# Another order for the first stage of a two-layer diffusion transformer: modulation, norm and first products ahead of the filters' taps and spectra, sums of squares in PSUM

## The chip, the core and the metric

The kernel runs on one core of a Trainium2 chip, in one launch. The metric is device time in microseconds (us), the median of 3 runs. Besides TensorE (PE; its weight loads are listed as PEld), the core has VectorE (DVE), ScalarE (ACT), GpSimd (POOL) and SyncE (SP), which here only issues DMAs. Each engine works through its own instructions in order and waits on semaphores. TensorE reads operands from SBUF and writes to eight banks of PSUM.

## The reference, cut to what matters

Two layers work on 256 latent tokens and 256 context tokens of 1024 features. What the first stage of the kernel computes is the beginning of layer 0 and the filters of both layers' long convolutions:

```python
cond_lat = jax.nn.silu(c)
cond_ctx = jax.nn.silu(c_ctx)[None]
m = adaln(cond_lat, ada_w[l], ada_b[l])        # 9 vectors of 1024: shift, scale, gate, ...
h = h + 0.5 * m[2] * swiglu(modulate(rms_norm(h), m[0], m[1]), ffn1_up[l], ffn1_down[l])
# rms_norm: x * rsqrt(mean(x * x) + eps); modulate: x * (1 + scale) + shift

# hyena_filter: a sine network of three layers, then taps, a window and a norm
hdn = jnp.sin(f_freq[0] * (z @ f_w1 + f_b[0]))
hdn = jnp.sin(f_freq[1] * (hdn @ f_w_mid[0] + f_b[1]))
hdn = jnp.sin(f_freq[2] * (hdn @ f_w_mid[1] + f_b[2]))
filt = (hdn @ f_w_out).reshape(length, 2, HY_W) * jnp.exp(-t * deltas)[:, None, :]
k_full = ...                                   # both directions
return k_full / jnp.sum(jnp.abs(k_full), axis=0, keepdims=True)
# fft_conv multiplies by rfft(k_full), the filter's spectrum
```

After that come the feed-forward block, four token mixers, a gated merge and a second feed-forward block, and all of it again for layer 1.

## The kernel before

Features lie on the partitions (8 tiles of 128), the 512 tokens of both streams along the free axis. A matrix product in full precision is made of three products (`mm3`, lines 250 to 252): weights and activations are split into a high part of reduced mantissa (`whi`, `nh`) and the remainder (`wlo`, `nl`). ScalarE casts the high part and VectorE subtracts for the low one (lines 224 and 225). Filters, sums and modulation use plain fp32 operands instead; every such product is recorded as two matmul records, two passes.

The first stage is the method `start`. It has five strands:
- **The filters' network** (`filter_layer`, lines 527 to 543): three small layers for both depths at once. Each is one product on TensorE, six operations on VectorE, and a sine on ScalarE.
- **Taps and spectra** (`filter_list`): per depth four taps (line 551; VectorE multiplies by the window, line 553), their sums and differences (`e`, line 562), five spectra of two products each (line 583; ScalarE copies them to `K`, line 585, and stores them to DRAM from its own queue, line 588), and the norm of the taps: absolute values on ScalarE (line 569), sums on GpSimd (line 571), four products with ones (line 574). `K` has two buffers.
- **Sums of squares**: ScalarE squares the eight feature tiles (line 1219), GpSimd adds them into `acc` (line 1221), and TensorE sums over partitions with four products by a column of ones (line 352). VectorE scales (line 344), GpSimd raises to the power -1/2 (line 345), and four products with the identity spread the factor over the partitions (line 357).
- **Modulation units** (`ada_unit`): 256 modulation columns each, from 1 MB of weights (`araw`, line 281). Eight narrow products (line 285), a copy (line 288), two products that add up the four partial sums (line 291), then the bias on VectorE (line 322). Units 4 to 7 make scales, units 0 to 3 shifts. The units 4+p and p belong to pair p of feature tiles.
- **Normalisation and first products**: `norm_pair` for pair p multiplies by the factor (`nt`, line 369), applies scale and shift on ScalarE (`nh`, line 374) and GpSimd (`nv`, line 375), and takes the difference on VectorE (`nl`, line 376). `mm3` then adds pair p's share to the two accumulators of the first feed-forward tile (`lead`): 24 products after p = 1 (pairs 0 and 1), 12 after p = 2 and 12 after p = 3.

In the code, the taps of both depths come first, and the spectra are written last. A scheduler places each engine's instructions by its own estimate of when their operands are ready, so the engine's sequence is not the code's; the sequences shown below are what it put out. PSUM's eight banks are shared out by kind: three for matmul (`mmb`), two for scores and spectra (`sb`), two for small results (`ptb`), one for unit sums (`ob`). SyncE issues the loads in the order of its own sequence, and a load waits for the buffer that it fills and for an earlier load's semaphore.

## Time and profile before

| | |
|---|---|
| median of 3 runs | 2556.85 us (2555.41 to 2559.32) |
| span of the profiled execution | 2554.3 us |
| TensorE busy | 2483.0 us, 97% of the span |
| VectorE, ScalarE, GpSimd busy | 59%, 39%, 13% |
| chain that ended last | PE 9%, issue 8%, DVE 2%, the rest 1% each or less |

The page has no time of the profiled execution other than its span; the span runs from the first to the last instruction. A busy share is an average: of the page's 40 slices (64 us each), all but the first show TensorE busy at 8 tenths or more, and the first shows 6. For that slice one looks at the engines' timelines. The page's clock digits are tenths of the full clock as far as the profiler has records of it.

### The profile page before, as it was taken

How to read it: one execution, taken by the hardware profiler on the slowest of the kernel's cores; microseconds unless marked ns; L12 is line 12 of the kernel's file. 1: busy time of each engine (PE TensorE's matmuls, PEld its weight loads, DVE VectorE, ACT ScalarE, POOL GpSimd, SP SyncE). 2: the span in 40 equal slices, each digit the busy share in tenths (PEclk: the TensorE clock that was granted, in tenths of full speed). 3: DMA queues.
4: the chain of work that ended last, by engine and by line, in shares of the span. 5: the costliest groups of instructions: out<-in, count | busy, mean ns of one | idle time of the engine just before them, and what ended most of it. 6: DMA issues, size and time to landing. Idle time of an engine off the chain costs nothing. (4 is left out here: it accounts for less than half of the span.)

```text
span 2554.3 us, 35123 instructions
## 1 busy us (share of the span) xinstructions
PE 2483.0 (97%) x13980; PEld 2092.7 (82%) x13980; DVE 1501.3 (59%) x2404; ACT 1004.1 (39%) x1767; POOL 320.7 (13%) x378
## 2 busy tenths in 40 slices
PE   6999999999999999999999999999999999899998
PEld 3788888876887777688888888888898898789998
DVE  5779865465465345557785355553356765556555
ACT  3422224455235434434222233222236545445443
POOL 3100001111113122212000010000021122221000
PEclk9999999999999999999999999999999999999999
DMA  7556544132212243333564234452243433545453
GB/s 268 207 182 229 190 167 147 57 92 81 97 38 87 64 108 91 102 123 139 187 219 168 73 133 182 163 199 92 81 141 108 160 124 91 124 130 189 148 202 113
DMA packets 82907, 350.99 MB, mean 137 GB/s; under 512 B 25206, under 2 KB 31032, under 8 KB 56632
## 3 DMA queue, kind: packets, MB, share of 16 engines
q1 hardware_dynamic: 81016, 345.61, 40.9%
q10 hardware_dynamic: 1728, 3.15, 0.3%
q8 instruction: 110, 1.80, 0.3%
q14 instruction: 53, 0.43, 0.1%
HBM read 333.52 MB, written 6.82 MB: 133 GB/s over the span
## 5 line engine op out<-in xcount | busy, mean ns | idle before, releaser
L250 PE MATMUL mmb<-nh,whi 128*128 128x512 f32 (+1 forms) x2224 | 788.5, 355 | 2.8 <-ACT nh L374 1.4
L251 PE MATMUL mmb<-nl,whi 128*128 128x512 f32 (+1 forms) x2224 | 786.0, 353 | 2.8 <-DVE nl L376 2.8
L252 PE MATMUL mmb<-nh,wlo 128*128 128x512 f32 (+1 forms) x2224 | 787.0, 354 | 1.1 <-DVE wlo L225 0.9
L224 ACT CAST whi<-raw 128x1024 fp32r<-128x1024 f32 (+4 forms) x532 | 474.3, 925 | 728.4 <-PE mmb L251 632.0
L225 DVE TENSOR_TENSOR wlo<-raw,whi 128x1024 fp32r<-128x1024 f32 (+4 forms) x532 | 582.3, 1117 | 151.7 <-ACT whi L224 134.5
L250 PEld LDWEIGHTS mmb<-nh,whi 128*128 128x128 f32 x2224 | 422.1, 190 | 65.6 <-issue 6.8
L251 PEld LDWEIGHTS mmb<-nl,whi 128*128 128x128 f32 x2224 | 421.9, 190 | 63.0 <-DVE nl L376 5.4
L252 PEld LDWEIGHTS mmb<-nh,wlo 128*128 128x128 f32 x2224 | 421.7, 190 | 63.0 <-issue 4.9
L251 PE MATMUL mmb<-pl,whi 128*128 128x512 f32 (+1 forms) x770 | 267.1, 347 | 0.0
L252 PE MATMUL mmb<-ph,wlo 128*128 128x512 f32 (+1 forms) x770 | 267.1, 347 | 0.0
L250 PE MATMUL mmb<-ph,whi 128*128 128x512 f32 (+1 forms) x770 | 266.8, 347 | 0.0
L430 DVE TENSOR_TENSOR s<-s,mmb 128x512 f32<-128x512 f32 (+1 forms) x85 | 52.7, 620 | 239.8 <-PE mmb L252 232.0
L314 DVE SCALAR_TENSOR_TENSOR vraw<-vraw,cb 128x1024 f32<-128x1024 f32 x128 | 155.6, 1224 | 36.2 <-DMA vraw<-in_adat 29.2
L345 POOL TENSOR_TENSOR rstd<-msq,nhalf 128x2 f32<-128x2 f32 (+1 forms) x11 | 8.4, 764 | 1308.5 <-DVE msq L344 1308.5
L251 PEld LDWEIGHTS mmb<-pl,whi 128*128 128x128 f32 x770 | 145.8, 189 | 18.2
L250 PEld LDWEIGHTS mmb<-ph,whi 128*128 128x128 f32 x770 | 145.8, 189 | 18.1
L252 PEld LDWEIGHTS mmb<-ph,wlo 128*128 128x128 f32 x770 | 145.8, 189 | 17.9
L314 DVE SCALAR_TENSOR_TENSOR scr<-vraw,cb 128x1024 f32<-128x1024 f32 x96 | 117.2, 1221 | 42.5 <-DMA vraw<-in_adat 36.9
L386 DVE SCALAR_TENSOR_TENSOR h<-mmb,mods,h 128x256 f32<-128x256 f32 x136 | 61.3, 480 | 129.9 <-PE mmb L252 129.8
L741 POOL TENSOR_SCALAR P<-P,rs 128x512 f32<-128x512 f32 (+1 forms) x144 | 92.2, 657 | 319.2 <-DVE rs L738 286.4
L429 ACT ACTIVATE s<-mmb 128x512 f32<-128x512 f32 (+1 forms) x85 | 46.3, 545 | 212.1 <-PE mmb L252 212.1
L252 PE MATMUL mmb<-whi,nl 128*128 128x256 f32 (+1 forms) x400 | 113.6, 284 | 0.9 <-DVE nl L376 0.7
(269 smaller groups left out, 3461.0 us busy)
## 6 DMA issues: line engine op xcount, KB each, us to landing
raw<-in_up SPq DMA_DIRECT2D x88, 1024.0 KB, 4.9
vraw<-in_adat SPq DMA_DIRECT2D x64, 1024.0 KB, 4.9
raw<-in_wmg SPq DMA_DIRECT2D x64, 768.0 KB, 4.5
raw<-in_dn SPq DMA_DIRECT2D x64, 704.0 KB, 4.1
raw<-in_wh SPq DMA_DIRECT2D x12, 1024.0 KB, 4.9
araw<-in_adaw SPq DMA_DIRECT2D x8, 1024.0 KB, 9.1
K<-K SPq DMA_DIRECT2D x64, 128.0 KB, 2.7
raw<-in_wnqk SPq DMA_DIRECT2D x8, 1024.0 KB, 4.9
```

The lines of the kernel that those rows point to most:

```text
L224: nc.scalar.copy(hi, src)
L225: nc.vector.tensor_tensor(lo, src, hi.bitcast(F32), ALU.subtract)
L250: nc.tensor.matmul(out, wh, xh, start=start and i == 0, stop=False)
L251: nc.tensor.matmul(out, wh, xl, start=False, stop=False)
L252: nc.tensor.matmul(out, wl, xh, start=False, stop=stop and i == n - 1)
L314: nc.vector.scalar_tensor_tensor(out, raw[:, j], 1.0, self.cb[:, s], ALU.mult, ALU.mult, accum_out=mc[:, j, s:s + 1])
L345: nc.gpsimd.tensor_tensor(out, ms[:, :n], self.nhalf[:, :n], ALU.pow)
L386: self.nc.vector.scalar_tensor_tensor(h[:, j, a:b], ps[:, a:b], self.mods[l][:, 8 * chunk + j, g:g + 1], h[:, j, a:b], ALU.mult, ALU.add)
L429: nc.scalar.activation(s[:, :n], pa[:, :n], AF.Silu)
L430: nc.vector.tensor_tensor(s[:, :n], s[:, :n], pg[:, :n], ALU.mult)
L741: nc.gpsimd.tensor_scalar(sl, sl, rs[:, qt:qt + 1], 0.0, ALU.mult, ALU.add)
```

## The change

The method `start` is written in another order, and three helpers are cut to fit it.
- The sums of squares no longer pass through GpSimd: each squared tile is multiplied by the column of ones at once, and the eight tiles add up in one bank of PSUM (32 products where there were 4). `rstd_bcast` is split, so that `start` can call its second half, `rstd_spread`, on that bank.
- The factor is spread before any taps. The modulation units of pair 0 follow, its normalisation, then the taps of depth 0, then pair 1 with the first products, and so on; taps and spectra of depth 1 come last. The two depths now share the taps' buffers (`f`, `e` without the depth in their name).
- Loads: the units' weights have four buffers of their own. The first two stand right behind the activations, the next two behind the taps' weights, then the first up weights and the table for the spectra. The constants of layer 1 are loaded last.

```diff
-    def ada_unit(self, i, u, pool, bufs):
+    def ada_load(self, i, pool, bufs):
         raw = pool.tile([128, 2048], F32, tag="raw", name="araw", bufs=bufs)
         r = raw.rearrange("p (k c) -> p k c", k=8)
-        nc.sync.dma_start(out=r, in_=self.a["adaw"][i])
+        self.nc.sync.dma_start(out=r, in_=self.a["adaw"][i])
+        return r
+
+    def ada_unit(self, r, u, pool):
...
-        ev = self.cp.tile([128, 256], F32, tag="adaev", name="adaev", bufs=2)
+        ev = pool.tile([128, 256], F32, tag="adaev", name="adaev", bufs=2)
...
+        return self.rstd_spread(wk, st, nb)
+
+    def rstd_spread(self, wk, st, nb):
...
-            f = fp.tile([128, 512], F32, name=f"f{l}{i}{d}")
+            f = fp.tile([128, 512], F32, name=f"f{i}{d}")
...
-                    st["eo"[q], i] = t = fp.tile([128, 512], F32, name=f"e{l}{i}{q}")
+                    st["eo"[q], i] = t = fp.tile([128, 512], F32, name=f"e{i}{q}")
...
         for j in range(0, KT, 2):
-            nc.sync.dma_start(out=h[:, j:j + 2], in_=self.a["xt"][:, j:j + 2])
+            nc.sync.dma_start(out=h[:, j:j + 2], in_=a["xt"][:, j:j + 2])
+        nc.sync.dma_start(out=self.small[0], in_=a["small"][0])
+        units = _ada_units()[0]
+        raws = [self.ada_load(i, sp, 4) for i in (4, 0)]
         self.filter_load_taps(fp, c)
-        for l in range(L):
-            nc.sync.dma_start(out=self.small[l], in_=self.a["small"][l])
+        raws += [self.ada_load(i, sp, 4) for i in (5, 1)]
         for i in range(3):
             self.filter_layer(fp, c, i)
+        st = self.tbank()
         for j in range(KT):
-            sq = sp.tile([128, T], F32, tag="sq", name="sq", bufs=2) if j else acc
+            sq = sp.tile([128, T], F32, tag="sq", name="sq", bufs=2)
             nc.scalar.activation(sq, h[:, j], AF.Square)
-            if j:
-                nc.gpsimd.tensor_tensor(acc, acc, sq, ALU.add)
-        fl = [f for pair in zip(*(self.filter_list(fp, l, c) for l in range(L))) for f in pair]
-        self.do(fl[:8])
-        units = _ada_units()[0]
+            for b in range(T // 128):
+                nc.tensor.matmul(st[:, b:b + 1], sq[:, 128 * b:128 * b + 128], self.ones[:, 0:1],
+                                 start=j == 0 and b == 0, stop=j == KT - 1 and b == T // 128 - 1)
+        bc = self.rstd_spread(wk, st, T // 128)
+        fl = [f for l in range(L) for f in self.filter_list(fp, l, c)]
         for p in range(4):
-            self.ada_unit(4 + p, units[4 + p][1], sp, 2)
-            self.ada_unit(p, units[p][1], *((self.wp, 3) if p % 2 else (sp, 2)))
-            if p == 0:
-                self.filter_load_dft(fp, c)
-                bc = self.rstd_bcast(wk, acc, 0, T)
             if p == 1:
-                wh, wl = self.load(self.a["up1"][0, 0], [2, 8, 128])
+                wh, wl = self.load(a["up1"][0, 0], [2, 8, 128])
                 lead = [self.bank(), self.bank()]
+                self.filter_load_dft(fp, c)
+            for i in (4 + p, p):
+                raw = raws.pop(0)
+                if p < 2:
+                    raws.append(None)
+                self.ada_unit(raw if raw is not None else self.ada_load(i, sp, 4), units[i][1], sp)
             for g, x, y in self.groups(T):
                 self.norm_pair(wk, bc[:, x:y], h, 0, 0, g, x, y, 2 * p)
+            self.do(fl[:4] if p == 0 else ())
             if p == 0:
-                self.do(fl[8:10])
                 continue
...
-        self.do(fl[10:])
+            self.do(fl[4 * p:4 * p + 4])
+        nc.sync.dma_start(out=self.small[1], in_=a["small"][1])
+        self.do(fl[16:])
         return [lead]
```

How this moves instructions on the engines shows in their sequences. The lines of the changed kernel are a few higher for the same operation. TensorE, from the last tap on, before: units are `ob`, spectra `sb<-e`, sums `ptb<-ones,acc`, the spread `ptb<-ident,rstd`.

```order
L551 MATMUL mmb<-fwo,hdn_171 128x512
L285 MATMUL ob<-araw,cond 32x256 x8
L583 MATMUL sb<-e_301,fdft 128x512
L291 MATMUL ptb<-ident,adaev 128x2 x2
L285 MATMUL ob<-araw,cond 32x256 x8
L583 MATMUL sb<-e_305,fdft 128x512
L291 MATMUL ptb<-ident,adaev 128x2 x2
L352 MATMUL ptb<-ones,acc 128x1 x4
L583 MATMUL sb<-e_309,fdft 128x512
L357 MATMUL ptb<-ident,rstd 128x128 x4
L583 MATMUL sb<-e_313,fdft 128x512
```

Seven more taps stand ahead of these rows. TensorE from its first product on, after (`ptb<-ones,sq` are the sums, `sb<-hdn` the filter layers, `mmb<-fwo` the taps):

```order
L535 MATMUL sb<-fzt,fw_118 128x256
L1233 MATMUL ptb<-ones,sq 128x1 x8
L535 MATMUL sb<-hdn,fwm 128x256
L1233 MATMUL ptb<-ones,sq 128x1 x16
L535 MATMUL sb<-hdn,fwm 128x256
L1233 MATMUL ptb<-ones,sq 128x1 x8
L365 MATMUL ptb<-ident,rstd 128x128 x4
L288 MATMUL ob<-araw,cond 32x256 x8
L294 MATMUL ptb<-ident,adaev 128x2 x2
L288 MATMUL ob<-araw,cond 32x256 x8
L294 MATMUL ptb<-ident,adaev 128x2 x2
L559 MATMUL mmb<-fwo,hdn_175 128x512 x4
```

The sums, now eight times as many, stand between the filter layers; the spread and two units come ahead of the first tap, and four of the eight taps are left for later.

TensorE around the first products (`mmb<-nh,whi`), before:

```order
L285 MATMUL ob<-araw,cond 32x256 x8
L583 MATMUL sb<-e_313,fdft 128x512
L291 MATMUL ptb<-ident,adaev 128x2 x2
L583 MATMUL sb<-e_303,fdft 128x512
L250 MATMUL mmb<-nh,whi 128x512
L251 MATMUL mmb<-nl,whi 128x512
L583 MATMUL sb<-e_307,fdft 128x512
L252 MATMUL mmb<-nh,wlo 128x512
L250 MATMUL mmb<-nh,whi 128x512
L251 MATMUL mmb<-nl,whi 128x512
```

The same place after:

```order
L288 MATMUL ob<-araw,cond 32x256 x8
L294 MATMUL ptb<-ident,adaev 128x2 x2
L288 MATMUL ob<-araw,cond 32x256 x8
L294 MATMUL ptb<-ident,adaev 128x2 x2
L591 MATMUL sb<-e_390,fdft 128x512
L250 MATMUL mmb<-nh,whi 128x512
L251 MATMUL mmb<-nl,whi 128x512
L252 MATMUL mmb<-nh,wlo 128x512
L250 MATMUL mmb<-nh,whi 128x512
L251 MATMUL mmb<-nl,whi 128x512
```

Before, ten products for spectra (`sb<-e`) stand ahead of or among the first 24 products; after, one. The first products now follow the second pair of units directly.

ScalarE ahead of the casts of the first weights (`whi`), before:

```order
L585 ACTIVATE K<-sb,kw 128x512 x2
L288 COPY adaev<-ob 128x256
L588 DMA kd_101<-K 128x512
L588 DMA kd_100<-K 128x512
L288 COPY adaev<-ob 128x256
L224 CAST whi<-raw 128x1024 x2
L374 ACTIVATE nh<-nt,mods_95 128x256 x4
```

The same after (`as` and `ab` are the absolute values of the taps):

```order
L291 COPY adaev<-ob 128x256
L577 ACTIVATE ab<-f_301 128x512
L291 COPY adaev<-ob 128x256
L382 ACTIVATE nh<-nt,mods_95 128x256 x3
L224 CAST whi<-raw 128x1024 x2
L382 ACTIVATE nh<-nt,mods_95 128x256
L593 ACTIVATE K<-sb,kw 128x512
```

Before, the casts stand ahead of the pair's four activations; after, behind three of them.

## Rows read from the trace of the kernel before

**Rows 1.** Windows: stretch, length, TensorE busy (records), clock, DMA share, GB/s.

```profile
0.00:21.94 21.94, 3.64 (x7) 1.00 0.87 316
21.94:40.15 18.21, 17.06 (x78) 0.96 0.49 171
```

**Rows 2.** Timeline of TensorE: start, duration, line, operation, shapes, records, idle before.

```profile
9.20 1.22 PE L527 MATMUL sb<-hdn,fwm 128*128 128x256 f32 x2 [4.16 <-ACT hdn L538]
21.94 8.67 PE L551 MATMUL mmb<-fwo,hdn 128*128 128x512 f32 x16 [3.93 <-ACT hdn L543]
30.54 1.07 PE L285 MATMUL ob<-araw,cond 128*32 128x256 f32 x16
35.71 1.03 PE L352 MATMUL ptb<-ones,acc 128*128 128x1 f32 x8
36.60 1.10 PE L583 MATMUL sb<-e,fdft 128*128 128x512 f32 x2
38.48 1.88 PE L357 MATMUL ptb<-ident,rstd 128*128 128x128 f32 x8 [0.77 <-POOL rstd L345]
49.07 0.80 PE L250 MATMUL mmb<-nh,whi 128*128 128x512 f32 x1
56.62 0.40 PE L252 MATMUL mmb<-nh,wlo 128*128 128x512 f32 x1
```

**Rows 3.** Timeline of TensorE's weight loads during the taps.

```profile
22.95 0.34 PEld L551 LDWEIGHTS mmb<-fwo,hdn 128*128 128x128 f32 x1 [0.52 <-issue]
25.29 0.19 PEld L551 LDWEIGHTS mmb<-fwo,hdn 128*128 128x128 f32 x1 [0.30 <-issue]
25.72 0.19 PEld L551 LDWEIGHTS mmb<-fwo,hdn 128*128 128x128 f32 x1 [0.24 <-issue]
```

**Rows 4.** Windows of TensorE around two falls of the clock.

```profile
36.00:38.70 2.70, 1.93 (x11) 1.00 1.01 413
38.70:42.10 3.40, 3.40 (x11) 0.50 0.99 373
2346.10:2350.00 3.90, 2.21 (x8) 0.50 0.40 90
```

**Rows 5.** Timeline of TensorE, a late sum at the lower clock.

```profile
2346.54 0.99 PE L352 MATMUL ptb<-ones,acc 128*128 128x1 f32 x4 [2.71 <-DVE acc L339]
```

**Rows 6.** Timeline of ScalarE, VectorE and GpSimd in the first stage.

```profile
7.70 0.63 ACT L1219 ACTIVATE acc<-h 128x512 f32<-128x512 f32 x1 [3.09 <-DMA h<-in_xt]
16.32 0.42 ACT L538 ACTIVATE hdn<-sx 128x256 f32<-128x256 f32 x1 [2.78 <-DVE sx L535]
41.12 2.08 ACT L374 ACTIVATE nh<-nt,mods 128x256 fp32r<-128x256 f32 x4 [4.88 <-DVE nt L369]
...
5.08 0.54 DVE L530 TENSOR_SCALAR sx<-sb,fbf 128x256 f32<-128x256 f32 x1 [3.26 <-PE sb L527]
7.24 0.29 DVE L535 TENSOR_SCALAR sx<-sx 128x256 f32<-128x256 f32 x1
10.46 0.54 DVE L530 TENSOR_SCALAR sx<-sb,fbf 128x256 f32<-128x256 f32 x1 [2.94 <-PE sb L527]
...
37.02 1.40 POOL L345 TENSOR_TENSOR rstd<-msq,nhalf 128x4 f32<-128x4 f32 x1 [3.97 <-DVE msq L344]
41.19 2.70 POOL L375 TENSOR_SCALAR nv<-nt,mods 128x256 f32<-128x256 f32 x4 [2.77 <-DVE nt L369]
```

**Rows 7.** Timeline of SyncE's queue, and the modulation loads' time to landing.

```profile
7.69 1.59 SPq L281 DMA_DIRECT2D araw<-in_adaw  x2
...
DMA to landing us min/median/max: 5.3/9.1/11.1
```

**Rows 8.** Timeline: casts and low halves of the first weights.

```profile
47.61 2.00 ACT L224 CAST whi<-raw 128x1024 fp32r<-128x1024 f32 x2
...
48.79 2.36 DVE L225 TENSOR_TENSOR wlo<-raw,whi 128x1024 fp32r<-128x1024 f32 x2
```

**Rows 9.** Waits of the first 110 us: us, times, longest.

```profile
ACT K L585 <- DMA kd<-K: 4.6, 3, 2.0
```

More of the change, by code (lines that the diff above doesn't have):

```diff
@@ L273, in tbank @@
         return self.pt.tile([128, 512], F32, tag="pt", name="ptb")
-    def ada_unit(self, i, u, pool, bufs):
-        nc = self.nc
+    def ada_load(self, i, pool, bufs):
         raw = pool.tile([128, 2048], F32, tag="raw", name="araw", bufs=bufs)
         r = raw.rearrange("p (k c) -> p k c", k=8)
-        nc.sync.dma_start(out=r, in_=self.a["adaw"][i])
+        self.nc.sync.dma_start(out=r, in_=self.a["adaw"][i])
+        return r
+    def ada_unit(self, r, u, pool):
+        nc = self.nc
         ps = self.obank()
@@ L352, in rstd_bcast @@
             nc.tensor.matmul(st[:, j:j + 1], acc[:, a + 128 * j:a + 128 * j + 128], self.ones[:, 0:1], start=True, stop=True)
+        return self.rstd_spread(wk, st, nb)
+    def rstd_spread(self, wk, st, nb):
+        nc = self.nc
         rs = wk.tile([128, 16], F32, tag="rstd", name="rstd", bufs=2)
@@ L358, in rstd_bcast @@
                              start=True, stop=True)
-        return tb[:, :b - a]
+        return tb[:, :128 * nb]
     def groups(self, n):
@@ L1223, in start @@
-        self.do(fl[:8])
-        units = _ada_units()[0]
+            for b in range(T // 128):
[3 more added lines that the diff above has]
+        fl = [f for l in range(L) for f in self.filter_list(fp, l, c)]
         for p in range(4):
-            self.ada_unit(4 + p, units[4 + p][1], sp, 2)
-            self.ada_unit(p, units[p][1], *((self.wp, 3) if p % 2 else (sp, 2)))
-            if p == 0:
+            if p == 1:
+                wh, wl = self.load(a["up1"][0, 0], [2, 8, 128])
+                lead = [self.bank(), self.bank()]
```

4 lines of the change are left out of this document (1 added, 3 removed).

## The prediction, made before the changed kernel had run

> **What bounds the kernel now.** First the page's shares: TensorE is busy for 97% of the span, so a change of the first stage can only win what TensorE idles there, and must not give it work. The windows of the first stage [rows 1] show the idle time: of the first 21.94 us TensorE works 3.64, of the next 18.21 it works 17.06. The timeline [rows 2] shows what it does: three layers of the filter network with long gaps, eight taps at 21.94, the modulation units from 30.54, the sums of squares at 35.71, the spread of the norm's factor at 38.48 to 40.36, the first products of the first feed-forward tile from 49.07. The last of the first 24 of these starts at 56.62 and the next row at about 56.9. From there nearly every slice is full, so I measure the change by that place: when do these 24 products end, and how much of the first stage's TensorE work is then still to come. TensorE's order after the first stage is the same in both kernels.
>
> **The clock comes into every price.** In the first 25 us TensorE runs at its lower level, 1.2 GHz: the same weight load takes 0.34 us at 22.95 and 0.19 at 25.29 [rows 3]. The window row of that stretch still prints a clock of 1.00 [rows 1]; the durations are to be believed. Later the granted clock reads 0.50 from 38.70 to 42.10 and again from 2346.10 [rows 4]. It rose at about 25 after 3 us of dense taps. It fell at 38.70 after a stretch in which TensorE had run mostly one-column products, one product for a spectrum and then idled.
>
> **What the sums of squares cost on TensorE.** Before, the eight squares are added on GpSimd and TensorE makes 4 products of one column (8 records). After, each of the eight squares gets its 4 products: 32, or 64 records. At the full clock a record takes 0.111 us: eight start at 35.71 and the next row at 36.60 [rows 2]. At the lower clock, four take 0.99 with their tail [rows 5]; the tail at the full clock is 1.03 - 0.89 = 0.14, so a record is (0.99 - 0.14)/4 = 0.2125; the nearest other row, the spread at 38.48 (128 columns out, nearly all at clock 0.50), takes 1.88 for eight, at most 0.235 each. The bounds for all 64 are thus 7.1 and 15.0 us. I take 13.6: they run from 8 to 24 us, where the clock is low now, and they are the very kind of product after which it fell. It is neither less than zero nor hidden: in before, these 8 records cost 0.9.
>
> The Trainium skill ("TensorE: Matmul & The Clock Gate", section "LDWEIGHTS (loading the stationary operand)") prices a weight load by its columns over 1.2, 107 ns for 128, with no second price for the lower clock. By it the 64 would cost 6.8 us and the sum below would come out near +2 us. The row at 2346.54 speaks for twice that; I keep the row, and the other outcome is the first rival.
>
> **The path after, step by step** (lower clock until the taps).
> 1. The first square is ready at 7.70 + 0.6 [rows 6]; the sums start at 8.4. TensorE takes 13.6 for them and two filter layers of 1.1 each between them: end 24.2. A square's buffer (two of them) is free as soon as its four products are done, so ScalarE keeps ahead.
> 2. The seven GpSimd additions go, and with them, as I read it, the slowdown of VectorE beside them: the second layer's chain took from 10.46 to its sine at 16.32, the first, undisturbed, 5.08 to 7.5 [rows 6]. It wins nothing: ScalarE's second sine now stands behind four squares that wait for TensorE, and comes at about 17.4 instead of 16.3.
> 3. Mean square 0.2, power on GpSimd 1.40 [rows 6], spread 1.88 [rows 2]: the factor is there at 27.9 instead of 40.4. That is the gain of the reorder, 12.5 us.
> 4. Two modulation units. A unit is 1.07 us at the full clock [rows 2], then ScalarE's copy and the way there 0.6, then 4 records, 0.45. At the lower clock I take 2.1 + 0.6 + 0.85, twice: 27.9 + 7.1 = 35.0. Their loads stand two places earlier in the queue than now; now they are issued at 7.69, and no unit's load took longer than 11.1 us to land [rows 7], so none is late.
> 5. Four taps, layer 0. A pass is 0.85 at the lower clock and 0.43 at the full one (25.29 to 25.72 [rows 3]); eight passes between 3.4 and 6.8, with the clock rising after some 3 us as at 25: 5.6. End 40.6. The first pair's normalisation (GpSimd 2.70 [rows 6]) lies beside them.
> 6. Two more units at the full clock, 2.1 each: 44.7, modulation columns ready at 45.0.
> 7. ScalarE's order puts three of the pair's four activations (2.08 for four [rows 6]) ahead of the two casts of the first weights (2.00 [rows 8]): first half cast at 47.6, second 48.6. VectorE has a difference and a product ahead of its two (2.36 for both): 49.1 and 50.3.
> 8. The products start at 47.6, where before it was 49.07; eight can run before the second low half is there, the other 16 take 16 x 0.23 = 3.7: end at 54.2. So the first products end 2.7 us **earlier** than now.
> 9. But TensorE has less behind it. Before that point it now has done all eight taps and ten products for spectra, each of two passes; after the change four taps and one product for spectra. Thirteen products of 0.86 move behind it: +11.2 us.
>
> Sum: -2.7 + 11.2 = +8.5. Bounds of this case: clock up already at the units -1 to -3; gaps where TensorE waits for the last low difference or a modulation column +0 to +1.5. So +5.5 to +10 by this walk, and I take +8.7. The same by work and idle: TensorE gets +12.7 for the sums, about +2.9 for two units at the lower clock and +0.4 for the taps; spectra that now run between 38.70 and 42.10 at the lower clock save about 1; it idles some 15.5 us up to the 24 products instead of 19.5 (18.3 and 1.15 by [rows 1]): +11. So +11 is this case's upper end.
>
> **At no cost:** the moved loads. On SyncE's queue the first up weights and the spectra's tables now stand ahead of the load that waits for the first unit's products (done at 30); with 11.1 us to land [rows 7] they are there by 41, and their first users come at 44.7 and 46.6. That cover is thin: a load later by 10 us would cost TensorE 5 at the first products. Taps of layer 1 now reuse layer 0's buffers and wait for its spectra; two further units and 12 products stand between.
>
> **Rivals.**
> - *The sums run at 0.111 a record.* Either the clock rises early in them or the weight loads don't follow the clock. The Trainium skill (same page, section "What's actually happening") says activity releases the throttle, and by that the unbroken stream of sums could release it. For it: TensorE is issuing nearly without a gap from 8.4 on. Against it: at 38.70 the clock fell right after such records. It would save 6.5 us on the sums, and, with the clock still up, up to 6 more on spread, units and taps: Δ from +2.2 down to -3.8, about 2553 to 2559. It decides from five of the eight squares on at the full clock (each saves 0.81, 4.1 in all): then the result is no longer slower beyond what can be measured.
> - *The clock falls a second time, and spectra wait for their stores.* Between 44.7 and 50.3 TensorE has one product for a spectrum and half of its first products; a like stretch ended in a fall at 38.70. Then 3.4 us run at half rate: +1.7. And layer 0's five spectra now follow one another, with two buffers whose stores ScalarE now waits for 3 times, 4.6 us in all, at most 2.0 [rows 9]; one copy of a modulation unit stands behind such a wait: 0 to +3. Together +10.5 to +13.5: 2567.3 to 2570.3.
> - *The reorder does as it looks*: first products early enough that TensorE idles much less (under 8 us up to the first products) and the time falls by over 0.2%. The gaps of steps 4 and 7 would have to vanish as well as half of the sums: the full-rate case's -3.8, less 2.4 for the copies' gaps of step 4 and 2.2 for step 7, is -8.4 or 2548.4. I see no row for it.
>
> **How the numbers follow.** The profiled span is 2554.3; the median is 2556.85, 2.55 above it (what lies around the span and run to run). 2554.3 + 8.7 + 2.55 = 2565.5. Chances: this case 0.60, second fall and stores 0.17, full-rate sums 0.19, the last 0.04. The measurement can tell about 0.2%, 5.1 us, from no change. This case lies above that except for its lower edge (0.03): slower 0.60 - 0.03 + 0.17 = 0.74; same 0.03 + 0.18 = 0.21; faster 0.05. The range reaches down to 2557, into the full-rate case (two thirds of it, 0.13, and the last case stay out), and up to 2569.5, over most of the second-fall case.
>
> **What would show it.** Right: 64 one-column records of 0.21 us between 8 and 24.5; the spread's end near 28; the first products at 47 to 48.5 and the 24th near 54; the first stage's TensorE rows then ending some 9 us later than now. Wrong at step 1 if the records are 0.11 apart; at step 4 or 5 if the weight loads read 0.19 before the taps; at step 7 if the casts come before the third activation's modulation columns; at step 9 if TensorE has gaps behind the first products. If the profile shows the sums hidden in time that TensorE idled anyway, with the factor at 20 instead of 28, the first rival holds.

## The result, and the profile after

The changed kernel takes **2570.88 us** (median of 4 runs, 2570.13 to 2572.41) against 2556.72 of the kernel before (4 runs, 2555.41 to 2559.32): ratio 1.0057, 95% interval 1.0045 to 1.0069, 14.2 us slower. Forecast was 2565.5 with a range of 2557.0 to 2569.5: the sign was right, the size was not, and the time lies above the range. The profiled spans are 2569.5 and 2554.3.

To find where the time comes in, take one product that both kernels have behind all of the filters' work: the 83rd product of the feed-forward block. It starts at 87.76 in before and at 102.22 after, 14.5 us later; from there on the difference stays between 14.0 and 16.3, and is 15.2 at the end. So the first stage has nearly all of it. I call this product **the mark**.

Windows of before, cut at its first tap, first product, end of the 24th product and the mark (length, TensorE busy with records, weight loads, VectorE, ScalarE, GpSimd, clock, DMA share, GB/s):

```profile
0.00:21.94 21.94, 3.64 (x7) 1.50 (x7) 12.06 (x23) 7.26 (x14) 9.13 (x11) 1.00 0.87 316
21.94:49.07 27.13, 25.98 (x131) 13.29 (x131) 16.83 (x32) 10.73 (x20) 8.34 (x9) 0.94 0.51 180
49.07:56.85 7.78, 7.08 (x28) 4.79 (x26) 5.15 (x7) 3.77 (x7) 4.58 (x4) 1.00 1.01 410
56.85:87.76 30.91, 30.43 (x176) 19.90 (x175) 12.89 (x23) 16.29 (x27) 9.55 (x11) 1.00 0.61 225
```

The same four of after:

```profile
0.00:34.02 34.02, 24.40 (x118) 20.34 (x119) 9.49 (x28) 8.61 (x16) 1.20 (x5) 1.00 0.83 311
34.02:49.22 15.20, 10.29 (x51) 4.36 (x51) 11.67 (x20) 7.68 (x15) 9.33 (x11) 0.82 0.68 256
49.22:57.24 8.02, 7.92 (x24) 5.90 (x25) 3.61 (x4) 1.40 (x2) 0.20 (x1) 0.71 0.17 71
57.24:102.22 44.98, 42.42 (x202) 24.71 (x200) 19.73 (x33) 20.55 (x34) 9.91 (x11) 1.00 0.49 176
```

Read the last rows first. The first products start at the same time (49.22 against 49.07) and the 24th ends 0.4 later; but behind it stand 202 records and not 176, 42.42 us of work and not 30.43. These 26 records are the thirteen products of the filters that the change moved behind. TensorE's idle time up to the mark (length less busy) falls only from 20.6 to 17.2 us, although 12.8 us of sums were put into the first window.

TensorE after, in order of time, for [rows 2, 5]:

```profile
8.48 3.58 PE L1233 MATMUL ptb<-ones,sq 128*128 128x1 f32 x16 [3.63 <-ACT sq L1231]
12.91 6.83 PE L1233 MATMUL ptb<-ones,sq 128*128 128x1 f32 x32
20.59 3.41 PE L1233 MATMUL ptb<-ones,sq 128*128 128x1 f32 x16
25.35 2.08 PE L365 MATMUL ptb<-ident,rstd 128*128 128x128 f32 x8 [1.35 <-POOL rstd L348]
27.36 1.94 PE L288 MATMUL ob<-araw,cond 128*32 128x256 f32 x16
...
34.02 5.07 PE L559 MATMUL mmb<-fwo,hdn 128*128 128x512 f32 x8
39.02 1.07 PE L288 MATMUL ob<-araw,cond 128*32 128x256 f32 x16
...
43.82 2.06 PE L591 MATMUL sb<-e,fdft 128*128 128x512 f32 x2
49.22 0.80 PE L250 MATMUL mmb<-nh,whi 128*128 128x512 f32 x1 [3.35 <-ACT whi L224]
...
57.01 0.40 PE L252 MATMUL mmb<-nh,wlo 128*128 128x512 f32 x1
...
79.21 1.13 PE L559 MATMUL mmb<-fwo,hdn 128*128 128x512 f32 x2 [0.85 <-DVE f L561]
...
84.22 0.50 PE L251 MATMUL mmb<-nl,whi 128*128 128x512 f32 x1 [1.71 <-DVE nl L384]
```

The sums take 0.21 us a record (6.83/32), the factor is spread at 27.43, the taps end at 39.09. At 43.82, behind the second pair's units, a product for a spectrum takes 2.06 us where it took 1.10 in [rows 2]: the clock has fallen, ahead of the wait. Then TensorE waits 3.35 us for the casts of the first weights, and ten of the 24 products are issued before the clock is up again. Windows of after around that fall:

```profile
36.80:43.84 7.04, 5.47 (x47) 2.67 (x45) 6.22 (x11) 3.04 (x6) 3.62 (x4) 0.99 0.38 136
43.84:54.08 10.24, 6.79 (x14) 3.78 (x15) 7.69 (x11) 3.97 (x6) 3.58 (x5) 0.51 0.64 248
54.08:60.00 5.92, 5.92 (x22) 3.90 (x21) 0.00 (x0) 0.69 (x1) 0.00 (x0) 1.00 0.02 8
```

What held up the casts shows on VectorE, GpSimd and ScalarE (after, for [rows 6, 8]):

```profile
41.90 1.70 DVE L570 TENSOR_TENSOR e<-f,f 128x512 f32<-128x512 f32 x1
43.52 1.23 DVE L327 TENSOR_SCALAR mods<-mods 128x4 f32<-128x4 f32 x1
44.66 1.88 DVE L570 TENSOR_TENSOR e<-f,f 128x512 f32<-128x512 f32 x3
46.47 0.15 DVE L325 TENSOR_TENSOR mods<-ptb,small 128x4 f32<-128x4 f32 x1
...
40.43 4.29 POOL L579 TENSOR_TENSOR as<-as,ab 128x512 f32<-128x512 f32 x3 [3.26 <-ACT ab L577]
...
46.65 1.58 ACT L382 ACTIVATE nh<-nt,mods 128x256 fp32r<-128x256 f32 x3 [3.43 <-DVE mods L325]
48.14 1.98 ACT L224 CAST whi<-raw 128x1024 fp32r<-128x1024 f32 x2
```

The last unit's columns are out of TensorE at 44, but their bias is added at 46.47, because the taps' sums and differences stand ahead of it on VectorE. The first of those takes 1.70 us and a multiplication of 128x4 takes 1.23 while GpSimd adds magnitudes; three more sums take 0.63 each once GpSimd is done. The activations wait for the columns, and the casts stand behind three of them.

### The profile page after: what moved, and what is told of

It reads as the page before. It is cut to its first block, busy times and chain, and to the rows that moved or that the text cites. A ratio compares the mean times of both kernels' runs of the same rounds, so it can differ in the third digit from the quotient of the medians.

```text
span 2569.5 us, 35225 instructions
## 1 busy us (share of the span) xinstructions
PE 2500.4 (97%) x14036; PEld 2107.0 (82%) x14036; DVE 1498.7 (58%) x2404; ACT 1005.9 (39%) x1767; POOL 309.9 (12%) x371
## 4 chain that ended last, share of the span: by engine, by line
PE 79%; issue 9%; DVE 4%; POOL 3%; DMA 2%; ACT 2%; SPq 0%; POOLq 0%; DVEq 0%; ACTq 0%
PE mmb L252 22%; PE mmb L250 22%; PE mmb L251 22%; PE ob L774 3%; PE s L730 2%; PE ptb L763 1%; DMA braw<-in_rpb 1%; DVE wlo L225 1%; POOL nv L383 1%; ACT whi L224 1%; POOL P L749 1%; DMA raw<-in_wmg 1%; PE sb L591 1%; PE sb L252 1%; PE s L739 1%
```

## The experiments

Sixteen kernels were run. The mark and TensorE's idle and busy time up to it come from one profiled execution of each, the ratio from runs beside the kernel before. The profiled execution need not be a typical one: its time lies 1.5 us over the kernel's median in after, 3.2 over in e2, 2.6 over in e5, and 2.9 under in e18. So differences of 2 or 3 us at the mark are not established by the table alone.

| kernel | median us | ratio to before, 95% | mark | idle | busy |
|---|---|---|---|---|---|
| before | 2556.72 | | 87.8 | 20.6 | 67.1 |
| after | 2570.88 | 1.0057 (1.0045 to 1.0069) | 102.2 | 17.2 | 85.0 |
| e1: before, sums in PSUM | 2563.12 | 1.0030 (1.0018 to 1.0043) | 93.5 | 12.9 | 80.6 |
| e2: after, sums on GpSimd | 2568.73 | 1.0053 (1.0039 to 1.0067) | 102.0 | 28.0 | 74.0 |
| e3: before, sums on VectorE | 2556.62 | 1.0006 (0.9997 to 1.0014) | 86.1 | 18.5 | 67.6 |
| e4: after, fewer magnitudes | 2569.24 | 1.0048 (1.0033 to 1.0063) | 99.8 | 14.3 | 85.5 |
| e5: before, loads and units first | 2566.85 | 1.0037 (1.0024 to 1.0050) | 96.7 | 23.2 | 73.5 |
| e6: after, clock raised first | 2573.19 | 1.0061 (1.0044 to 1.0078) | 100.2 | 13.5 | 86.7 |
| e7: after, first weights earlier | 2566.43 | 1.0040 (1.0025 to 1.0054) | 95.0 | 13.2 | 81.9 |
| e8: after, filters' order undone | 2569.11 | 1.0048 (1.0033 to 1.0063) | 98.3 | 13.9 | 84.5 |
| e11: before, first weights earlier | 2562.20 | 1.0022 (1.0013 to 1.0031) | 92.6 | 23.3 | 69.3 |
| e12: e11 and e3 | 2561.95 | 1.0019 (1.0010 to 1.0028) | 93.6 | 19.8 | 73.8 |
| e13: after, load order undone | 2571.20 | 1.0060 (1.0046 to 1.0074) | 102.3 | 18.7 | 83.6 |
| e15: e13 and e7 | 2572.07 | 1.0061 (1.0047 to 1.0074) | 101.3 | 18.5 | 82.8 |
| e16: e2 and e7 | 2565.56 | 1.0038 (1.0025 to 1.0052) | 96.1 | 23.4 | 72.7 |
| e17: e8 and e7 | 2567.93 | 1.0045 (1.0031 to 1.0059) | 98.4 | 13.6 | 84.8 |
| e18: e2, e8 and e7 | 2568.30 | 1.0046 (1.0034 to 1.0059) | 94.3 | 23.3 | 71.0 |
| e19: after, products in the wait | 2568.61 | 1.0055 (1.0040 to 1.0070) | 99.0 | 14.0 | 85.0 |

The kernel before ran beside each of them again (medians 2555.1 to 2557.0), so ratios are to be compared rather than medians. No kernel is faster than before. The theory at the start: the sums on TensorE and the work moved behind the first products cost the time, each its own part. The rival: the order alone does it, wherever the sums are made.

### Are the sums on TensorE the cost?

```diff
...
+        st = self.tbank()
         for j in range(KT):
-            sq = sp.tile([128, T], F32, tag="sq", name="sq", bufs=2) if j else acc
+            sq = sp.tile([128, T], F32, tag="sq", name="sq", bufs=2)
             nc.scalar.activation(sq, h[:, j], AF.Square)
-            if j:
-                nc.gpsimd.tensor_tensor(acc, acc, sq, ALU.add)
+            for b in range(T // 128):
+                nc.tensor.matmul(st[:, b:b + 1], sq[:, 128 * b:128 * b + 128], self.ones[:, 0:1],
+                                 start=j == 0 and b == 0, stop=j == KT - 1 and b == T // 128 - 1)
...
```

Done alone in before (e1):

> The kernel before, with one part of the change alone: the sums of squares go through 32 one-column products into PSUM instead of seven GpSimd additions and 4 products. Path theory (the records cost only by what they push back on the way to the taps): 64 records of 0.21 us between 8 and 24 us, taps from about 24 instead of 21.94, the 4 old products gone: +1 to +3 us on the kernel before. Work theory (TensorE is 97% busy, so all its added work shows at the end): +12.7 us.

Undone alone in after (e2):

> The changed kernel with the sums of squares as before (seven GpSimd additions, 4 products); order and loads stay changed. Path theory: the factor's spread ends near 23.5 instead of 27.4, so about 4 us less than the changed kernel, still some 10 above the kernel before: the order costs that. Work theory: 12.7 us of TensorE work go, so the time comes within 2 or 3 us of the kernel before.

In before they cost 5.7 us at the mark and 7.4 in the median (2563.12 against 2555.72 beside it). That lies between the two theories. TensorE puts sixteen of the 64 records ahead of the second filter layer and 32 ahead of the third, and the first tap slips from 21.94 to 25.59. In after they cost 0.3 at the mark, less than either theory said. Windows of e2 with the same cuts as above:

```profile
0.00:32.68 32.68, 13.19 (x62) 8.05 (x63) 13.81 (x28) 8.50 (x16) 10.27 (x12) 1.00 0.88 324
32.68:48.51 15.83, 10.01 (x51) 4.31 (x51) 11.79 (x20) 7.68 (x15) 9.33 (x11) 0.96 0.66 246
48.51:56.93 8.42, 8.31 (x24) 6.20 (x25) 3.61 (x4) 1.40 (x2) 0.20 (x1) 0.67 0.15 64
56.93:101.95 45.02, 42.45 (x202) 24.75 (x200) 19.72 (x33) 19.97 (x33) 9.92 (x11) 1.00 0.51 176
```

Without the sums TensorE works 11.2 us less in the first window and idles 9.9 more: the factor needs GpSimd's additions about as long (spread's end 26.08 against 27.43). So in the new order the 64 records are nearly free, and of the 14.5 us the order, with its loads, makes 14.2: 7.3 more idle time than before, and 6.9 more busy time on the same products, most of it work at 1.2 GHz (a unit takes 1.94 us where before's took 1.07 in [rows 2]). This speaks for the rival.

A small test of what GpSimd's additions cost VectorE in before (e3):

```diff
-                nc.gpsimd.tensor_tensor(acc, acc, sq, ALU.add)
+                nc.vector.tensor_tensor(acc, acc, sq, ALU.add)
```

> The kernel before, with the seven additions of squares on VectorE instead of GpSimd. If GpSimd's additions slow VectorE's filter chain beside them (5.8 us for the second layer against 2.45 for the first): the chain falls back to some 2.5 us, the additions fit its gaps, taps start near 18 instead of 21.94, and the time falls by 3 to 4 us. If something else made the chain slow: seven additions of 0.7 us lengthen it, 0 to +3 us.

The taps come at 19.70, 2.2 us earlier where the first theory said 4, and the mark comes 1.7 us earlier, but of the time nothing can be told (1.0006, 0.9997 to 1.0014).

### Does the clock make the sums dear?

```diff
+        wz = sp.tile([128, 256], F32, name="wz")
+        nc.vector.memset(wz, 1.0)
+        wp = self.bank()
+        for i in range(10):
+            nc.tensor.matmul(wp[:, 0:256], self.ones, wz, start=True, stop=True)
         c = self.filter_load(fp)
```

> The changed kernel with ten more products of 256 columns on a tile of ones at the very start of TensorE's work; nothing reads their result. They take at most 8.5 us at the lower clock, in time that TensorE otherwise idles, up to 9 us. Theory A (the sums of squares cost 0.21 us a record only because the clock has not risen by then, and would hold a raised clock): weight loads of the sums read 0.11 a record, the factor's spread ends 4 to 6 us earlier than 27.4, and the units and taps behind it run at full rate; the common product comes 6 to 12 us earlier than after, 2559 to 2565. Theory B (one-column products let the clock fall again, as at 38.70 in before): sums at 0.11 for some microseconds, then 0.21 again; the common product gains 0 to 3 us, 2568 to 2571.

TensorE of e6:

```profile
1.60 6.68 PE L1222 MATMUL mmb<-wz,ones 128*128 128x256 f32 x20 [1.60 <-DVE wz L1219]
...
8.84 5.32 PE L1238 MATMUL ptb<-ones,sq 128*128 128x1 f32 x40
...
15.02 5.12 PE L1238 MATMUL ptb<-ones,sq 128*128 128x1 f32 x24
```

Its windows up to the rise, the fall and the next rise of the clock:

```profile
0.00:5.90 5.90, 4.29 (x10) 3.49 (x11) 1.25 (x6) 1.50 (x2) 0.19 (x4) 1.00 0.40 98
5.90:12.70 6.80, 6.80 (x47) 5.90 (x47) 2.28 (x6) 3.31 (x6) 0.00 (x0) 1.00 1.01 399
12.70:26.40 13.70, 12.23 (x60) 9.97 (x59) 4.81 (x13) 2.32 (x5) 1.12 (x1) 0.50 1.01 414
```

While the clock is up the sums are 0.11 us apart; at 12.70, in the middle of forty of them without a gap, it falls, and the last 24 take 5.12/24 = 0.213 each. The Trainium skill ("TensorE: Matmul & The Clock Gate", section "What's actually happening") says that activity releases the throttle; here it came back among products that followed one another without a pause. The spread ends at 23.66, 3.8 us earlier, the mark comes 2.1 earlier, which is theory B, and the time is no better (the median, 2573.19, lies above both theories). From the mark on, this profile loses 5.3 us against after with no fall in its records that after lacks; why stays open.

### Is it the filters' order, the loads, or both?

e5 takes the load order alone into before; units 4 and 0 and the sums then move ahead of the taps by themselves, while the spread stands among the last of them:

```diff
...
+        nc.sync.dma_start(out=self.small[0], in_=self.a["small"][0])
+        raws = [self.ada_load(i, sp, 2) for i in (4, 0)]
         self.filter_load_taps(fp, c)
-        for l in range(L):
-            nc.sync.dma_start(out=self.small[l], in_=self.a["small"][l])
+        raws += [self.ada_load(i, self.wp, 3) for i in (5, 1)]
...
```

> The kernel before with the change's order of loads alone: the modulation weights of the first two units right behind the activations, those of the next two behind the taps' weights, layer 1's constants last. Sums of squares stay on GpSimd, filters and spectra stay in before's order in the code. The instruction order then shows the first two units, the sums and the spread ahead of the taps by themselves. Theory A (what costs is that one-column products, spread and units come before the dense taps, so TensorE does them at 1.2 GHz and the clock rises later): spread near 26, taps from about 31, clock up at 34, a common product behind the first stage 5 to 9 us later than before; time 2561 to 2566. Theory B (what costs is the filters' order, half of the taps and ten spectra moved behind the first products, so that no filler is left in the waits): here the filters are whole, so the common product moves by less than 3 us, time 2555 to 2559.

e8 takes the filters' order back out of after:

```diff
...
-        fl = [f for l in range(L) for f in self.filter_list(fp, l, c)]
+        fl = [f for pair in zip(*(self.filter_list(fp, l, c) for l in range(L))) for f in pair]
...
-            self.do(fl[:4] if p == 0 else ())
+            self.do(fl[:10] if p == 0 else ())
...
-            self.do(fl[4 * p:4 * p + 4])
...
-        self.do(fl[16:])
+        self.do(fl[10:])
```

> The changed kernel with the filters' part of the change undone: all eight taps and both depths' sums and differences in the first pass of the loop, the spectra of both depths interleaved at the end of the code and free to fill TensorE's waits, a buffer for each depth; two buffers for the modulation weights and two of the weights' pool, as before. Sums in PSUM, loads and units first stay changed. Theory A (what costs is that too little filler is left beside the waits of the second pair, so that TensorE idles and its clock falls): TensorE full from the taps to the first products, no fall at 44 to 54, first products end later but the common product 4 to 7 us earlier than after, 2563 to 2566. Theory B (what costs is work at the lower clock ahead of the taps): the common product within 2 us of after, 2568 to 2571.

e5 is 8.9 us late at the mark, with the filters whole, as its theory A has it (the median, 2566.85, is just above the theory's, and the spread, which it wanted near 26, ends at 39.79): its first tap comes at 29.80 and not 21.94, and 6.4 of the 8.9 are busy time on the same products. e8 wins 3.9 of after's 14.5; the clock still falls, from 47.4 to 54.2. Taken one by one, the loads with the units ahead of the taps would be some 9 us, and the halved filters 4 to 5 (3.9 by e8, 14.2 - 8.9 = 5.3 by e2 and e5); these are differences of single profiles, and the next run shows that the two are not separate. At the mark e8 stands just under its theory A, in the median at B.

e13 puts the taps ahead of the units again, by the load order, with the filters halved:

```diff
-        nc.sync.dma_start(out=self.small[0], in_=a["small"][0])
-        raws = [self.ada_load(i, sp, 4) for i in (4, 0)]
         self.filter_load_taps(fp, c)
-        raws += [self.ada_load(i, sp, 4) for i in (5, 1)]
+        nc.sync.dma_start(out=self.small[0], in_=a["small"][0])
+        raws = [self.ada_load(i, sp, 4) for i in (4, 0, 5, 1)]
```

> The changed kernel with before's order of loads for the modulation units: their weights behind the taps' weights and the constants. The instruction order then has the four taps directly behind the factor's spread, and the first two units behind the taps. Theory A (after's taps stand ready at 26.5, when the last sine is written, and are late only because the spread and two units are ahead of them on TensorE; that keeps TensorE idle and at 1.2 GHz until 37): taps from 27.5 to 28.5, clock up at 30 to 32, units at full rate, a common product behind the first stage 4 to 7 us earlier than in after, 2564 to 2567. Theory B (the order of taps and units among themselves is worth nothing, since the second pair's columns and the casts end last either way): taps early, then a longer wait and fall ahead of the first products; common product within 2 us of after, 2568 to 2571.

The taps come at 26.75, 7.3 us earlier than in after, and nothing of it is left at the mark (102.33). That is theory B. TensorE and VectorE of e13:

```profile
36.16 1.07 PE L288 MATMUL ob<-araw,cond 128*32 128x256 f32 x16
40.84 1.01 PE L294 MATMUL ptb<-ident,adaev 128*128 128x2 f32 x4 [3.60 <-ACT adaev L291]
...
48.08 0.80 PE L250 MATMUL mmb<-nh,whi 128*128 128x512 f32 x1 [2.81 <-ACT whi L224]
...
32.76 1.55 DVE L570 TENSOR_TENSOR e<-f,f 128x512 f32<-128x512 f32 x1
34.24 0.15 DVE L325 TENSOR_TENSOR mods<-ptb,small 128x4 f32<-128x4 f32 x1
34.31 1.69 DVE L570 TENSOR_TENSOR e<-f,f 128x512 f32<-128x512 f32 x1
```

Its windows around the fall:

```profile
30.10:40.40 10.30, 6.15 (x61) 2.87 (x59) 8.64 (x13) 4.49 (x9) 6.35 (x6) 1.00 0.59 207
40.40:54.00 13.60, 9.81 (x36) 6.47 (x37) 7.15 (x12) 4.73 (x9) 3.55 (x6) 0.50 0.87 331
```

Now the taps' sums stand ahead of the first units' columns on VectorE; the wait moves to 36 to 48, and the fall lasts 13.6 us. I read this as follows, and no run shows it by itself: with half of the filters TensorE has nothing dense to do there, wherever the four taps stand.

### Is it the wait for the first products?

```diff
         raws = [self.ada_load(i, sp, 4) for i in (4, 0)]
+        wh, wl = self.load(a["up1"][0, 0], [2, 8, 128])
             if p == 1:
-                wh, wl = self.load(a["up1"][0, 0], [2, 8, 128])
```

> The changed kernel with the load of the first up weights put ahead of the second pair's units instead of behind them in the code, so that ScalarE's casts stand ahead of the second pair's activations and the first pair's products directly behind the taps. Theory A (the second fall of the clock at 43.84 and the idle time up to 49.22 come from the first products waiting for casts and the second pair's columns): first product near 41 to 43, no fall or a later one, the common product 4 to 6 us earlier than after, 2564 to 2567. Theory B (the columns of the second pair end last whatever the casts do): products of pair 0 earlier, those of pair 1 where they are, idle time moved but not won, fall still there: 0 to 2 us, 2568 to 2571.

The casts start at 33.60 and the first product at 39.28, but the clock falls twice ahead of the first products' end (length, TensorE busy with records, clock, DMA share, GB/s):

```profile
33.60 1.97 ACT L224 CAST whi<-raw 128x1024 fp32r<-128x1024 f32 x2
39.28 1.42 PE L250 MATMUL mmb<-nh,whi 128*128 128x512 f32 x1
...
31.72:35.13 3.41, 3.41 (x6) 0.50 0.99 404
38.54:41.96 3.42, 3.42 (x13) 0.50 0.00 0
```

The mark comes 7.2 us earlier, more than theory A said, and the median falls by 4.4 us, within theory A; its "no fall or a later one" does not hold. Of the 7.2, 2.3 are there at the first tap already (31.73 and not 34.02), where the clock had risen at 28.3 in this execution and at 36.8 in after; whether the edit has to do with that no run shows. From the mark on the profile loses 3.2 against before, most of it around 2240, where a stretch at the lower clock is 13.7 us long, against 10.2 in after and 6.8 in before. With the sums on GpSimd as well (e16):

> The changed kernel with the first up weights behind the first two units' weights, and the sums of squares added on GpSimd as before. Theory A (of the 7.3 us at the common point that the earlier weights alone leave against before, the sums in PSUM are 4 to 6, because they hold up the filter layers behind them on TensorE): common point at 88 to 91, 2557 to 2561. Theory B (the sums cost nothing there, GpSimd's additions take as long; what is left is the order, units at 1.2 GHz ahead of the taps): 94 to 97, 2564 to 2568.

Again the sums' place is worth nothing (mark 96.1 against 95.0, ratio 1.0038 against 1.0040): theory B. And against e2, whose first tap comes at the same time (32.76 and 32.68), the earlier weights gain 5.9 at the mark. The two remedies put together with others do not add:

> The changed kernel with both the former edit (units' weights behind the taps' weights and constants) and the first up weights ahead of the second pair's units. Theory A (the two waits are separate: taps behind the units, and first products behind casts and second columns): gains add, 5 and 7 us at the common product, so 90 to 92 us there, against 88 in before and 102 in after; 2559 to 2563. Theory B (both repair the same wait, which is TensorE without dense work between 27 and 49): no more than the better of the two, 94 to 96 there, 2564 to 2567. With sums in PSUM this kernel has 12.8 us more to do on TensorE than before, so it should not beat before.

> The changed kernel with the filters' order undone (eight taps in the first pass, spectra of both depths at the end) and the first up weights behind the first two units' weights; sums in PSUM. Theory A (filler and earlier weights are separate gains, 3.9 and 7.2 us at the common point): 91 to 92.5 there, 2559 to 2563. Theory B (both fill the same wait between the taps and the second pair's columns): 94 to 97, 2564 to 2568.

> The changed kernel with whole filters, earlier first weights and sums of squares on GpSimd: of the change, the loads of the units and the units ahead of the taps stay. Theory A (sums, filler and earlier weights are separate costs): common point at 86 to 90, 2554 to 2559, level with before. Theory B (units ahead of the taps at 1.2 GHz, with taps from 30 on, cost 5 us or more whatever else is done): 92 to 97, 2561 to 2567.

At the mark e17 and e18 are at their theory B or a little above it, and e15, which also writes the four taps ahead of the sums in the code, is worse than either of its theories: with the up weights' load issued later than in e7, TensorE waits 4.78 us for the casts. The medians of e15 and e18 lie above both theories, that of e17 at the upper edge of theory B. e17 has no fall of the clock between 37.7 and 92.4; but at 90.75 TensorE has waited 1.95 us for GpSimd's sum of magnitudes, and the clock falls from 92.4 to 95.8. So e17's mark does not show what whole filters and earlier weights are worth ahead of the 24 products. And in before, where TensorE has no such wait, a like edit makes it worse:

> The kernel before with the load of the first up weights ahead of all modulation units in the code, so that the first pair's products come among the spectra. Theory A (before is full from its first tap at 21.94 on; only the waits of 2 us and a fall of 3.4 us at 38.70 are there to be won): common product 0 to 2.5 us earlier, 2554 to 2556, no difference that can be told. Theory B (the first weights push the units' weights back in SyncE's queue and the units' columns come later): common product 1 to 4 us later, 2557 to 2560.

> The kernel before with the first up weights ahead of all units, and the sums of squares added on VectorE and not on GpSimd. Theory A (both gains add: taps at 19.7 and not 21.94, no fall ahead of the first products): common product at 83.5 to 85.5 against 87.8 in before, 2552 to 2554.5, the lowest time so far. Theory B (TensorE's idle time only moves behind the taps): common product at 86 to 88, 2555 to 2557.

The first product of e11 starts 2.9 us earlier than in before, and the mark comes 4.9 later: 2.6 of it is idle time, 1.6 of that at one place (VectorE's low difference at 76.54), the other 2.2 is busy time that I did not trace further. That is past theory B. e12 misses both of its theories: its taps start as early as in e3, at 19.66, but the clock is low from 34.7 to 41.5 and again at 89.3.

### What do the slowed VectorE and the fall cost by themselves?

In the norm of the taps (e4):

```diff
-            for n in range(4):
+            for n in range(1):
```

> The changed kernel, with three of the four magnitudes of each depth's norm left out (three ScalarE activations and three GpSimd additions per depth; the filters' norm is then that of one quarter). If these additions make the unforeseen part (VectorE's sums and differences of taps at 1.7 us instead of 0.7 with a modulation column behind them, and GpSimd's normalisation behind an addition at 78): the second pair's columns come at about 45 instead of 46.6, the waits of TensorE at 79 and 84 (0.85 and 1.71 us) shrink, -3 to -5 us. If not, within 1 us of the changed kernel.

The first product comes 1.8 us earlier, and the wait for VectorE at 84.22 is gone (idle behind the 24th product 1.0 and not 2.6); the mark gains 2.4, a little less than forecast. The last unit's bias comes at 44.63 and not 46.47, so the 1.8 is the collision on VectorE. The wait of 0.85 at the last tap stays. In this profile the 24 products took 9.0 us, with the clock low again. e19 fills the wait ahead of the first products:

```diff
+        self.ev = ev
...
+            if p == 1:
+                wf = self.sbank()
+                for i in range(7):
+                    nc.tensor.matmul(wf[:, 0:256], self.ones, self.ev, start=True, stop=True)
```

> The changed kernel with seven more products of 256 columns on the last unit's copy, between the second pair's units and the first products, where TensorE idles for some 3 us and its clock falls; nothing reads them. They take 3.1 us at the full clock. Theory A (the fall at 43.84 comes from this wait, and costs the 24 products and the spectrum 2.5 to 3 us): no fall up to 54, first product at 49 to 49.5, products 0.23 apart, common point at 99 to 100.5 against 102.2, 2567.5 to 2569.5. Theory B (the clock falls all the same, or the extra products end behind the casts): common point within 1 us of after or later, 2570 to 2573.

The extra products of e19 (14 records), two stretches of its TensorE (length, busy with records, clock, DMA share, GB/s), and the window from the first product to the end of the 24th:

```profile
42.01 4.95 PE L1251 MATMUL sb<-adaev,ones 128*128 128x256 f32 x14
...
32.29:35.70 3.41, 3.41 (x5) 0.50 1.03 377
42.53:45.94 3.41, 3.41 (x10) 0.50 1.00 393
...
47.49:53.96 6.47, 6.47 (x26) 4.86 (x27) 3.61 (x4) 1.40 (x2) 0.21 (x1) 1.00 0.18 73
```

The clock falls all the same, from 42.5 to 45.9, among the extra products, which take 4.95 us and not 3.1; it is up again ahead of the first product. So the fall does not come from the wait (in after, too, it is there ahead of it), and the "no fall up to 54" of theory A fails. But all 24 run at the full clock, with a spectrum of 0.9 among them: 5.6 us where after's took 8.0. So running them at the lower clock costs 2.4. The mark comes 3.3 earlier. Of this 1.9 is not the edit's: in this execution the clock rose at 28.9 and not at 36.8, with the same rows ahead of it (and fell again from 32.3 to 35.7), and the first tap came at 32.11. Against before, the gain can't be told from scatter (1.0055 against 1.0057).

## Why the prediction came out too low, by its own steps

- **Steps 1 to 5 were right** in their sizes: the sums take 0.2135 a record and end at 24.0 (24.2 forecast), the spread ends at 27.43 (27.9), the units at 34.0 (35.0), the taps at 39.09 (40.6), with the clock up at 36.8. The first rival, sums at 0.111, fell; in e6, where they began at the full clock, it fell among them. The Trainium skill's 107 ns for a weight load of 128 columns ("TensorE: Matmul & The Clock Gate", section "LDWEIGHTS (loading the stationary operand)") lies near the 0.111 us from record to record in e6 at the full clock; at the lower clock the record of 0.2135 is twice that.
- **Step 6 failed by 1.6 us.** The units left TensorE at 43.96 (44.7 forecast), but their columns were ready at 46.6 and not 45.0: the taps' sums on VectorE were not counted in the chain, nor that the magnitudes' additions on GpSimd now fall just beside them (e4, with one magnitude instead of four, has them at 44.8). It had the rows for it: the longer second chain of [rows 6], which it had read itself as a slowdown beside the squares' additions.
- **Step 7 was right in the order** (three activations ahead of the casts) and late by about the same, 1.5: casts from 48.14.
- **Step 8 failed by 3.0 us.** The 24th product ends at 57.24 and not 54.2: 1.6 from the first product (49.22 against 47.6), and 1.4 because the 24 products took 8.0 us and not 6.6. This second part is the fall of the clock. The prediction had a fall here as a rival, joined to late stores, with a chance of 0.17. It looked for it behind an empty stretch from 44.7 on, with 3.4 us at half rate and a price of 1.7. It came at about 43.7, behind the second pair's units with TensorE busy for 5.47 of the 7.04 us ahead of it, lasted 10.2 us, and cost the 24 products 2.4 (e19). What set it off stays open: products in the wait did not prevent it (e19), and e17, where taps and first products stand among the units, had none there. The stores, the other half of that rival, cost nothing that I could see.
- **Step 9 was right in kind and 2.9 too small.** Thirteen products did move behind: 26 records, 12.0 us and not 11.2. In addition TensorE idles 2.1 us more there, for VectorE at 79.21 and 84.22, while GpSimd adds the second depth's magnitudes; without three of the four magnitudes the second of these waits is gone (e4). The prediction had said that gaps there would prove it wrong.

Sum: -2.7 + 3.0 = +0.3 (0.4 by the rows) and 11.2 + 2.9 = 14.1, together 14.5 at the mark against 8.5; the rest of the kernel adds 0.7 in the profile.

The prediction's second reckoning, by work and idle time, had +11. It counted the sums, the units and the idle time rightly (14.6 us of idle time up to the 24th product, forecast 15.5) and lacked the fall and the gaps. The forecast went by the lower of the two sums; but the higher one, 2567.9, lies below the result too. **What failed are three terms: the columns' way over VectorE (1.6), the fall (1.4) and the gaps behind the first products with the dearer records there (2.9)**, 5.9 together. The range ended at 2569.5, inside the prediction's own second-fall case.

The reasons behind the sum were weaker than the sum. It counted the sums of squares as 12.7 us of added work. e2 and e16 show that their place is worth nothing in the new order: what they fill, TensorE would have idled. What costs, by e2's rows, is 7.3 us of idle time and 6.9 us of slower work on the same products. Why the order does this is my reading of the sequences, and is shown only in part: it takes dense work away from the waits. Before, eight taps and ten products for spectra lay beside the wait for factor, columns and casts; after, four taps and one such product do, more of the work there runs at the lower clock, and the rest of the dense work stands where TensorE has no wait to fill. The earlier factor, 13 us, bought nothing: the first products start where they did. An earlier load of the first weights, and with it earlier casts, gets back 4.4 us of the median (e7), and 5.9 to 7.2 at the mark (e16, e7). How much of the rest is due to the units ahead of the taps stays open: e5 and e18 show it only with other things moving too, since the scheduler reorders the engines at each edit, and e13, with the taps ahead of the units, gains nothing.

## What to carry to other kernels

On an engine that is full, an earlier start of one chain wins only if the waits on that chain are filled with other work; count what is dense and ready in each wait before and after, not only when the chain ends. The price of added work depends on where it lands: the same 12.8 us of sums cost 0.3 us at the mark in the new order, where TensorE would have idled (e2), and 5.7 in the old, where they put off the taps (e1). Where two reckonings of one change differ, the difference is a term that one of them lacks, and it is worth finding before choosing.

## What the runs showed of the hardware

- Among one-column products that followed one another without a pause, 0.11 us apart, the clock fell from 2.4 to 1.2 GHz at 12.70, and they were 0.213 apart from there (e6).
- The clock's rise comes at different times in executions with the same rows ahead of it: 36.8 in after, 28.9 in e19. The Trainium skill ("TensorE: Matmul & The Clock Gate", section "What's actually happening") says that the number of slow products varies from run to run; here it moves the first tap by 1.9 us, so single profiles should not be compared closer than that.
- A VectorE sum of 128x512 took 1.70 us while GpSimd added, and 0.63 alone; a 128x4 multiplication took 1.23 and 0.17. The Trainium skill ("Trainium Architecture — The Big Picture", section "What this means for kernel authors") says that only the port pair that the two share contends, and that it is an exclusive lock; the rows agree with it as far as they go: the multiplication ends at 44.75, and GpSimd's three additions at 44.72.
